# A hybrid encoder layer: the second pair's substitution, its values and the attention's projections in another order, the projection in three parts

## The chip, the cores and the metric

The kernel runs on one core of a Trainium2 chip. The metric is the device time of one execution in microseconds (us); the kernel before takes 1764.89 us, the median of three runs between 1764.22 and 1765.56.

The engines that matter are TensorE (PE in the profile, its weight loads PEld), VectorE (DVE), ScalarE (ACT), GpSimd (POOL) and SyncE (SP), which issues nearly all of this kernel's DMAs. Each engine carries out its own instructions strictly in the order in which the program lists them, and so does each queue of DMA issues: an instruction that waits holds up all that is listed behind it on its engine.

## What is computed

One layer of an encoder, applied with the same weights to a prompt of 1024 tokens and a sample of 256 (1280 tokens, ten tiles of 128). After a norm, one projection feeds two head groups. Group A is a bidirectional gated DeltaNet with four heads; group B is grouped-query attention with four query heads and two key-value heads, with a norm and an axial rotary position on queries and keys.

```python
h = _rmsnorm(x, norm_mix_pre)
p = h @ w_in
qkv_a, z_a, b_f, b_b, a_f, a_b, q_b, k_b, v_b = _split_cols(p)
o_a = _gated_deltanet(qkv_a, z_a, b_f, b_b, a_f, a_b, ...)
o_b = _axial_gqa(q_b, k_b, v_b, q_norm_w, k_norm_w)
mix = jnp.concatenate([o_a, o_b], axis=-1) @ w_out
x = x + _rmsnorm(mix, norm_mix_post)
hm = _rmsnorm(x, norm_mlp_pre)
f = jnp.square(jax.nn.relu(hm @ w_up)) @ w_down
return x + _rmsnorm(f, norm_mlp_post)
```

Inside the DeltaNet, every chunk needs a triangular solve, `tri = eye + strict(k_beta k^T * decay)`, per head, chunk and direction. The kernel builds the inverse of each triangle: 32x32 blocks on the diagonal by substitution, row by row, and then the blocks off the diagonal by small matmuls.

## The kernel before

All products are made in three matmuls of high and low parts (`hi*hi`, `hi*lo`, `lo*hi`), so one projection of 128 columns over 1280 tokens (`proj_T`, L351 to L369) is 72 matmuls: 48 of 512 columns and 24 of 256, in three blocks of tokens, each of which ends with a copy of its PSUM tile to SBUF by ScalarE (L369).

The execution has these stages: the norm and the z gate's projection; the **preparation** of DeltaNet and attention, from about 105 to 571 us of the trace; the DeltaNet's steps with the attention beside them, 571 to 799 us; the output projection; and the MLP, to the end.

In the preparation, generators are advanced one after the other by a string, `ORDER`. A letter names a generator and a digit its head, pair or projection; each mention runs it up to its next `yield`:

- `K0`..`K3`, `gdn_qk`: two projections, convolution, transposes and norms of a head's queries and keys.
- `V0`..`V3`, `gdn_v`: the same for its values.
- `E0`..`E3`, `gdn_e`: decay factors and k k^T products of a head, five pairs of chunks. It fills the matrix `C` and writes `A` (one buffer, L538) to DRAM (L544, L545).
- `S0`, `S1`, `gdn_sub`: the substitution of heads 0 and 1, or 2 and 3. It starts with a round trip of the diagonal blocks through DRAM (`c_d`, L564 to L567); then come 31 pairs of a product (L575, tile `prod`) and an update (L577, tile `Rm`) on VectorE, each dependent on the one before, with a memset on GpSimd (L578).
- `L0`..`L3`, `gdn_lev`: a head's blocks off the diagonal. It takes `Rm` through DRAM (`r_d` L585, `Rc` L589), transposes it on VectorE (`Rt` L592) and makes two levels of small matmuls (L605 to L617, L634 to L641); the finished `C` goes to DRAM (L645, L646).
- `a0`..`a7`, `att_proj`: the attention's projections, four of queries (`a0`..`a3`), two of keys (`a4`, `a5`), two of values (`a6`, `a7`). `a0`..`a5` write the projection to DRAM (L390) and load it back with halves of its rows exchanged (`axw`, four DMAs, L393); ten transposes (L399) feed sums of squares on ScalarE (L375); VectorE makes the reciprocal root in 13 small steps (L89 to L99) and four multiplications with the rotary table (L414 on the projection, L415 on `axw`); GpSimd adds the two (L416); keys are scaled by ten small matmuls (`prk`, L422) and VectorE (L425); the result goes to DRAM (L429).

The order in the string gives each instruction its place; the program's scheduler then orders the instructions of each engine by it, so neighbours in the string are interleaved.

Several buffers are few, and a step that needs one waits until its last user is done. The projection's result `araw` and the convolution's input share two buffers (tag `cp`, L387). `axw` and the convolution's output share one (tag `cy`). `A` has one. Three PSUM tiles serve all projections (`mm`). The buffers of the preparation as a whole (`gp`) are given up only when its last instruction has read them; the loads of the DeltaNet's steps (`vis`, L668) take the same memory.

Of the kernel before, what the change touches and what calls it, by code (L numbers as in the profile page):

```python
# [37 lines left out]


ORDER = (  # L40
# [3 lines left out]
)  # L44


# [16 lines left out]
def build(ctx, tc, I, O):  # L63
# [19 lines left out]
    def rsqrt(p, out, ss, n, inv_n, tag, x_out=None):  # L83

        x = x_out if x_out is not None else p.tile([128, n], F32, tag=f"{tag}x", name=f"{tag}x")
        xh = p.tile([128, n], F32, tag=f"{tag}h", name=f"{tag}h")
        y = p.tile([128, n], F32, tag=f"{tag}y", name=f"{tag}y")
        t = p.tile([128, n], F32, tag=f"{tag}t", name=f"{tag}t")
        V.tensor_scalar(x, ss, inv_n, EPS, ALU.mult, ALU.add)  # L89
        V.tensor_scalar(xh, x, -0.5, None, ALU.mult)  # L90
        V.tensor_scalar(t.bitcast(I32), x.bitcast(I32), 1, None, ALU.logical_shift_right)
        V.tensor_scalar(y.bitcast(I32), t.bitcast(I32), -1.0, MAGIC, ALU.mult, ALU.add)
        for i in range(3):
            if n == 1:
                V.scalar_tensor_tensor(t, y, xh, y, ALU.mult, ALU.mult)
            else:
                V.tensor_tensor(t, y, y, ALU.mult)
                V.tensor_tensor(t, t, xh, ALU.mult)
            V.scalar_tensor_tensor(out if i == 2 else y, t, 1.5, y, ALU.add, ALU.mult)  # L99
# [253 lines left out]
    def proj_T(c, dst, segs):  # L353
        wts = []
        for g in range(2):
            raw = tp_.tile([128, 4, 128], F32, tag="wraw", name="wraw", bufs=2)
            SP.dma_start(out=raw, in_=w_in[g * 512:(g + 1) * 512, c:c + 128].rearrange("(k p) c -> p k c", p=128))
            whi = tp_.tile([128, 4, 128], F32R, tag="whi", name="whi", bufs=3)
            wlo = tp_.tile([128, 4, 128], F32R, tag="wlo", name="wlo", bufs=3)
            split(whi, wlo, raw)  # L360
            wts.append((whi, wlo))
        for t0, n, c0 in segs:
            pm = mm_tile("pt")
            for k in range(KD):
                whi, wlo = (w[:, k % 4] for w in wts[k // 4])
                T.matmul(pm[:, :n], lhsT=whi, rhs=h_hi[:, k, t0:t0 + n], start=(k == 0), stop=False)  # L366
                T.matmul(pm[:, :n], lhsT=whi, rhs=h_lo[:, k, t0:t0 + n], start=False, stop=False)  # L367
                T.matmul(pm[:, :n], lhsT=wlo, rhs=h_hi[:, k, t0:t0 + n], start=False, stop=(k == KD - 1))  # L368
            S.copy(dst[:, c0:c0 + n], pm[:, :n])  # L369

    def sum_sq(p, tp, n, ss):

        for j in range(n):
            junk = p.tile([128, 128], BF16, tag="gj", name="gj", bufs=1)
            S.activation(junk, tp[:, j * 128:(j + 1) * 128], AF.Square, accum_out=ss[:, j:j + 1])  # L375
# [3 lines left out]
    def att_proj(j):  # L379

        if not att and j < 6:
            rope = gp.tile([128, 2, 1282], F32, tag="qk", name="rope", bufs=2)[:, :, 0:1024]
            SP.dma_start(out=rope, in_=I["c_rope"])
            att[0] = rope
        rope = att.get(0)
        c = (2064 + j * 128, 2576 + (j - 4) * 128, 2832 + (j - 6) * 128)[max(0, j - 2) // 2]
        raw = tp_.tile([128, TOK], F32, tag="cp", name="araw", bufs=2)  # L387
        proj_T(c, raw, ((0, 512, 0), (512, 512, 512), (1024, 256, 1024)))
        if j < 6:
            SP.dma_start(out=aqkv_d[j], in_=raw)  # L390
            xw = tp_.tile([128, TOK], F32, tag="cy", name="axw", bufs=1)
            for b in range(4):
                SP.dma_start(out=xw[b * 32:b * 32 + 32], in_=aqkv_d[j][(b ^ 1) * 32:(b ^ 1) * 32 + 32])  # L393
        yield
        for t0 in range(0, NT, 4):
            n = min(4, NT - t0)
            tp = at_tile("at")
            for i in range(n):
                T.transpose(tp[:, i * 128:(i + 1) * 128], raw[:, (t0 + i) * 128:(t0 + i + 1) * 128], ident)  # L399
            if j < 6:  # L400
                sum_sq(gp, tp, n, ssa[:, j, t0:t0 + n])
            else:
                cs = slice(t0 * 128, (t0 + n) * 128)
                vn = gp.tile([128, 512], F32, tag="kn", name="avn", bufs=3)[:, :n * 128]
                S.copy(vn, tp[:, :n * 128])
                SP.dma_start(out=arot_d[j][:, cs], in_=vn)
        if j >= 6:
            return
        rs = rsa[:, j]
        rsqrt(gp, rs, ssa[:, j], NT, 1.0 / 128, "na")  # L410
        w = nw[:, j // 4]
        for c0, n in ((0, 1024), (1024, 256)):
            cs = slice(c0, c0 + n)
            V.scalar_tensor_tensor(raw[:, cs], raw[:, cs], w[:, 0:1], rope[:, 0, :n], ALU.mult, ALU.mult)  # L414
            V.scalar_tensor_tensor(xw[:, cs], xw[:, cs], w[:, 1:2], rope[:, 1, :n], ALU.mult, ALU.mult)  # L415
        G.tensor_tensor(raw, raw, xw, ALU.add)  # L416
        if j >= 4:
            for t0 in range(0, NT, 4):
                n = min(4, NT - t0)
                pr = at_tile("prk")  # L420
                for i in range(n):
                    T.matmul(pr[:, i * 128:(i + 1) * 128], lhsT=rs[:, t0 + i:t0 + i + 1].to_broadcast([128, 128]), rhs=ident,  # L422
                             start=True, stop=True)
                cs = slice(t0 * 128, (t0 + n) * 128)
                V.tensor_tensor(raw[:, cs], raw[:, cs], pr[:, :n * 128], ALU.mult)  # L425
        else:
            V.tensor_scalar(rs, rs, scale, None, ALU.mult)
            V.tensor_scalar(nsa[:, j], rs, -1.0, None, ALU.mult)
        SP.dma_start(out=arot_d[j], in_=raw)  # L429
# [152 lines left out]
    def gdn_lev(h):  # L582
# [63 lines left out]
        SP.dma_start(out=vis_d[h][:, :, 8], in_=C[:, :, 0])  # L646

    FN = dict(K=gdn_qk, V=gdn_v, E=gdn_e, S=gdn_sub, L=gdn_lev, a=att_proj)
    parts = {}
    for step_ in ORDER.split():  # L650
# [666 lines left out]
    for s, (n, i) in enumerate(seq):  # L1317
# [20 lines left out]
        if s > 9 and (s - 10) % 4 == 0 and s < 38:  # L1338
            j = UP[(s - 10) // 4][1]
# [171 lines left out]
```

## Time and profile before

| | us |
|---|---|
| median of three runs | 1764.89 (1764.22 to 1765.56) |
| the profiled execution, its own time | 1767.37 |
| its span in the trace | 1765.6 |
| outside the span | 1.8 |
| PE busy in the span | 1633.7 (93%) |
| DVE busy | 1244.3 (70%) |
| ACT busy | 875.8 (50%) |
| POOL busy | 697.8 (40%) |

The profile is one execution. Its page gives busy times over the whole span; the windows view gives busy time of each engine in a stretch of time, with the clock that TensorE was granted (1 is full speed); the timeline gives single instructions, with the idle time before one and what ended it in brackets; the groups view sums instructions of one line and kind; the waits view lists who waited for whom. A line number such as L575 is one of the kernel before, unless the changed kernel is spoken of: there the lines of `att_proj` from L395 on, and all behind it, have moved by up to two.

### The profile page before, as it was taken

How to read it: one execution, taken by the hardware profiler on the slowest of the kernel's cores; microseconds unless marked ns; L12 is line 12 of the kernel's file. 1: busy time of each engine (PE TensorE's matmuls, PEld its weight loads, DVE VectorE, ACT ScalarE, POOL GpSimd, SP SyncE). 2: the span in 40 equal slices, each digit the busy share in tenths (PEclk: the TensorE clock that was granted, in tenths of full speed). 3: DMA queues.
4: the chain of work that ended last, by engine and by line, in shares of the span. 5: the costliest groups of instructions: out<-in, count | busy, mean ns of one | idle time of the engine just before them, and what ended most of it. 6: DMA issues, size and time to landing. Idle time of an engine off the chain costs nothing. (4 is left out here: it accounts for less than half of the span.)

```text
span 1765.6 us, 27828 instructions
## 1 busy us (share of the span) xinstructions
PE 1633.7 (93%) x9799; PEld 1401.9 (79%) x9799; DVE 1244.3 (70%) x2425; ACT 875.8 (50%) x2017; POOL 697.8 (40%) x574
## 2 busy tenths in 40 slices
PE   6999998997856999989998999999989999999997
PEld 5778887776744878767877899999988788888885
DVE  6557559736857687886668955544777888887777
ACT  5237747565226676775446654545556333333422
POOL 3201011101114243530001465445635777888663
PEclk9999999998877999999999999999999999999999
DMA  6113434255444876444333444343565544444334
GB/s 208 66 45 108 132 84 121 73 150 152 139 126 135 276 234 205 135 152 141 128 111 127 160 165 144 127 136 129 184 210 194 171 145 135 135 141 138 98 111 154
DMA packets 208778, 252.67 MB, mean 143 GB/s; under 512 B 35073, under 2 KB 163391, under 8 KB 208639
## 3 DMA queue, kind: packets, MB, share of 16 engines
q1 hardware_dynamic: 208495, 250.77, 44.7%
q8 instruction: 77, 1.26, 0.3%
q14 instruction: 62, 0.51, 0.1%
q0 software_dynamic: 144, 0.13, 0.0%
HBM read 159.75 MB, written 91.10 MB: 142 GB/s over the span
## 5 line engine op out<-in xcount | busy, mean ns | idle before, releaser
L1162 PE MATMUL pd<-mh,ulo 128*128 128x320 f32 x892 | 280.1, 314 | 12.9 <-DVE ulo L81 12.9
L1161 PE MATMUL pd<-mh,uhi 128*128 128x320 f32 x892 | 277.1, 311 | 5.0 <-ACT uhi L80 5.0
L1163 PE MATMUL pd<-ml,uhi 128*128 128x320 f32 x892 | 277.6, 311 | 0.0
L1305 DVE TENSOR_TENSOR acc<-acc,pd 128x512 f32<-128x512 f32 x330 | 206.8, 679 | 43.9 <-PE pd L1301 43.9
L1299 PE MATMUL pd<-dhi,fhi 128*128 128x512 f32 x490 | 192.4, 393 | 1.4 <-DVE acc L1307 1.4
L1300 PE MATMUL pd<-dl,fhi 128*128 128x512 f32 x490 | 192.5, 393 | 0.0
L1301 PE MATMUL pd<-dhi,flo 128*128 128x512 f32 x490 | 192.0, 392 | 0.0
L1162 PEld LDWEIGHTS pd<-mh,ulo 128*128 128x128 f32 x892 | 169.6, 190 | 17.9 <-DVE ulo L81 17.9
L366 PE MATMUL pt<-h_hi,whi 128*128 128x512 f32 (+1 forms) x480 | 177.1, 369 | 0.0
L367 PE MATMUL pt<-h_lo,whi 128*128 128x512 f32 (+1 forms) x480 | 175.6, 366 | 0.0
L368 PE MATMUL pt<-h_hi,wlo 128*128 128x512 f32 (+1 forms) x480 | 175.1, 365 | 0.4 <-DVE wlo L81 0.4
L1161 PEld LDWEIGHTS pd<-mh,uhi 128*128 128x128 f32 x892 | 169.4, 190 | 6.3 <-ACT uhi L80 6.2
L1163 PEld LDWEIGHTS pd<-ml,uhi 128*128 128x128 f32 x892 | 169.5, 190 | 0.0
L1281 ACT CAST fhi<-fr 128x1280 fp32r<-128x1280 f32 x49 | 62.1, 1268 | 212.1 <-PE pd L1300 116.6
L81 POOL TENSOR_TENSOR dl<-dw,dhi 128x1024 fp32r<-128x1024 f32 x49 | 129.0, 2632 | 43.4 <-ACT dhi L80 42.8
L1206 POOL TENSOR_TENSOR s<-u,u 128x320 f32<-128x320 f32 x32 | 35.5, 1108 | 208.6 <-ACT u L1171 141.8
L743 POOL TENSOR_TENSOR P<-P,sm 128x512 f32<-128x512 f32 (+1 forms) x72 | 72.6, 1027 | 96.5 <-DVE sm L741 67.4
L1299 PEld LDWEIGHTS pd<-dhi,fhi 128*128 128x128 f32 x490 | 92.0, 188 | 22.6 <-DVE acc L1307 1.9
L81 DVE TENSOR_TENSOR ulo<-us,uhi 128x512 fp32r<-128x512 f32 x88 | 77.9, 887 | 43.9 <-ACT uhi L80 43.1
L1301 PEld LDWEIGHTS pd<-dhi,flo 128*128 128x128 f32 x490 | 92.0, 188 | 20.8
L1300 PEld LDWEIGHTS pd<-dl,fhi 128*128 128x128 f32 x490 | 92.0, 188 | 20.4
L368 PEld LDWEIGHTS pt<-h_hi,wlo 128*128 128x128 f32 x480 | 91.8, 191 | 15.0 <-DVE wlo L81 0.9
(358 smaller groups left out, 4092.0 us busy)
## 6 DMA issues: line engine op xcount, KB each, us to landing
fr<-r_d SPq DMA_DIRECT2D x49, 640.0 KB
vis<-vis_d SPq DMA_DIRECT2D x64, 384.0 KB
uraw<-in_w_up SPq DMA_DIRECT2D x22, 1024.0 KB
r_d<-s SPq DMA_DIRECT2D x128, 160.0 KB
r_d<-u SPq DMA_DIRECT2D x96, 160.0 KB
dw<-in_w_down SPq DMA_DIRECT2D x28, 512.0 KB
wraw<-in_w_in SPq DMA_DIRECT2D x48, 256.0 KB
x<-in_x_prompt SPq DMA_DIRECT2D x16, 512.0 KB
```

Of the source, the lines that this page charges most:

```text
L81: (V if leng is None else leng).tensor_tensor(lo, src, f32(hi), ALU.subtract)
L366: T.matmul(pm[:, :n], lhsT=whi, rhs=h_hi[:, k, t0:t0 + n], start=(k == 0), stop=False)
L367: T.matmul(pm[:, :n], lhsT=whi, rhs=h_lo[:, k, t0:t0 + n], start=False, stop=False)
L368: T.matmul(pm[:, :n], lhsT=wlo, rhs=h_hi[:, k, t0:t0 + n], start=False, stop=(k == KD - 1))
L743: G.tensor_tensor(x[:, :kw], x[:, :kw], sm[:, 0:1].to_broadcast([128, kw]), ALU.mult)
L1161: T.matmul(pm, lhsT=w[0][:, k], rhs=mh[b, i][:, k], start=(k == 0), stop=False)
L1162: T.matmul(pm, lhsT=w[1][:, k], rhs=mh[b, i][:, k], start=False, stop=False)
L1163: T.matmul(pm, lhsT=w[0][:, k], rhs=ml[b, i][:, k], start=False, stop=(k == 3))
L1299: T.matmul(pm, lhsT=r[0][:, k, tk], rhs=w[0][:, k], start=(k == 0), stop=False)
L1300: T.matmul(pm, lhsT=r[0][:, k, tk], rhs=w[1][:, k], start=False, stop=False)
L1301: T.matmul(pm, lhsT=r[1][:, k, tk], rhs=w[0][:, k], start=False, stop=(k == Q - 1))
L1305: V.tensor_tensor(half(t, d), half(t, d), pm, ALU.add)
```

## The change

Two things are changed: the string `ORDER`, and the places at which `att_proj` yields.

```diff
@@ -38,9 +38,9 @@
 ORDER = (
-    "K0 K0 K0 V0 K0 K0 V0 E0 K1 E0 V0 E0 E0 K1 E0 K1 a6 K1 K1 a6 E1 a7 E1 E1 a7 E1 E1 V1 S0 K2 S0 V1 S0 K2 S0 V1 S0 K2 "
-    "S0 K2 S0 K2 S0 K3 L0 L0 K3 L1 L1 E2 V2 E2 K3 E2 K3 E2 V2 K3 E2 V2 V3 E3 E3 V3 E3 a4 E3 V3 E3 a4 S1 a5 S1 a5 S1 a0 "
-    "S1 S1 a0 S1 a1 S1 S1 a1 L2 L2 a2 L3 L3 a2 a3 a3"
+    "K0 K0 K0 V0 K0 K0 V0 E0 K1 E0 V0 E0 E0 K1 E0 K1 a6 K1 K1 a6 E1 E1 V1 E1 E1 E1 S0 K2 S0 V1 S0 K2 S0 V1 S0 K2 "
+    "S0 K2 S0 K2 S0 K3 L0 L0 K3 L1 E2 L1 K3 a7 E2 E2 K3 E2 K3 E2 a7 E3 V2 E3 E3 V2 E3 E3 S1 V2 V3 S1 S1 V3 S1 a4 S1 "
+    "V3 S1 a4 S1 a5 S1 a4 L2 a5 L2 a0 L3 a5 L3 a0 a1 a0 a1 a2 a1 a2 a3 a2 a3 a3"
 )
@@ -388,10 +388,11 @@
         proj_T(c, raw, ((0, 512, 0), (512, 512, 512), (1024, 256, 1024)))
         if j < 6:
             SP.dma_start(out=aqkv_d[j], in_=raw)
+        yield
+        if j < 6:
             xw = tp_.tile([128, TOK], F32, tag="cy", name="axw", bufs=1)
             for b in range(4):
                 SP.dma_start(out=xw[b * 32:b * 32 + 32], in_=aqkv_d[j][(b ^ 1) * 32:(b ^ 1) * 32 + 32])
-        yield
         for t0 in range(0, NT, 4):
             n = min(4, NT - t0)
             tp = at_tile("at")
@@ -406,6 +407,7 @@
                 SP.dma_start(out=arot_d[j][:, cs], in_=vn)
         if j >= 6:
             return
+        yield
         rs = rsa[:, j]
         rsqrt(gp, rs, ssa[:, j], NT, 1.0 / 128, "na")
         w = nw[:, j // 4]
```

`att_proj` has now three parts for queries and keys: the projection and its write to DRAM; the load of `axw`, the transposes and the sums of squares; and the reciprocal root, the rotary multiplications, the scaling and the write. In the string, `a7` goes from amid `E1` to behind `K3`; the pairs of `E2` and `E3` follow one another with `V2` begun only inside `E3`; `S1` stands with `V2`, `V3`, `a4` and `a5` instead of `a5`, `a0` and `a1`; and `a5` to `a3` are staggered behind and between `L2` and `L3`. The number of instructions on each engine is the same before and after (8823 on PE, 2427 on DVE, 1707 on ACT, 579 on POOL, 825 on SP, as the programs list them).

On VectorE, around the eighth to tenth step of `S1` (`prod` and `Rm` are the substitution's product and update; `araw`, `axw` and `prk` are the attention projection's), the kernel before has these instructions:

```order
L575 TENSOR_TENSOR prod<-Rm 80x2x192
L415 SCALAR_TENSOR_TENSOR axw<-axw,nw,rope 128x1024
L415 SCALAR_TENSOR_TENSOR axw<-axw,nw,rope 128x256
L577 TENSOR_TENSOR Rm<-Rm,prod 80x2x24x8
L575 TENSOR_TENSOR prod<-Rm 80x2x207
L577 TENSOR_TENSOR Rm<-Rm,prod 80x2x23x9
L425 TENSOR_TENSOR araw<-araw,prk 128x512 x2
L425 TENSOR_TENSOR araw<-araw,prk 128x256
L575 TENSOR_TENSOR prod<-Rm 80x2x220
L81 TENSOR_TENSOR wlo<-wraw,whi 128x512
L577 TENSOR_TENSOR Rm<-Rm,prod 80x2x22x10
L414 SCALAR_TENSOR_TENSOR araw<-araw,nw,rope 128x1024
```

and the changed kernel these, from the eighth step to the twelfth:

```order
L577 TENSOR_TENSOR prod<-Rm 80x2x192
L579 TENSOR_TENSOR Rm<-Rm,prod 80x2x24x8
L577 TENSOR_TENSOR prod<-Rm 80x2x207
L579 TENSOR_TENSOR Rm<-Rm,prod 80x2x23x9
L577 TENSOR_TENSOR prod<-Rm 80x2x220
L579 TENSOR_TENSOR Rm<-Rm,prod 80x2x22x10
L417 SCALAR_TENSOR_TENSOR axw<-axw,nw,rope 128x1024
L577 TENSOR_TENSOR prod<-Rm 80x2x231
L417 SCALAR_TENSOR_TENSOR axw<-axw,nw,rope 128x256
L579 TENSOR_TENSOR Rm<-Rm,prod 80x2x21x11
L577 TENSOR_TENSOR prod<-Rm 80x2x240
L427 TENSOR_TENSOR araw<-araw,prk 128x512
```

Before, the rotary work of `a4`, `a5`, `a0` and `a1` stands inside `S1`; in the changed kernel only one rotary step on `axw` and one scaling, both of `a4`, and later a rotary step of `a5`. Of GpSimd's adds (L416, in the changed kernel L418), three stand inside `S1` before and one after.

On SP's queue, around the end of `S1` (`r_d` carries the substitution's result to DRAM, `Rc` brings it back for `L2` and `L3`, `arot_d` is a finished projection, `ax` the attention's own loads), the kernel before has these issues:

```order
L429 DMA arot_d<-araw 128x1280
L393 DMA axw<-aqkv_d 32x1280 x4
L390 DMA aqkv_d<-araw 128x1280
L429 DMA arot_d<-araw 128x1280
L393 DMA axw<-aqkv_d 32x1280 x2
L585 DMA r_d<-Rm 80x1024
L393 DMA axw<-aqkv_d 32x1280
L589 DMA Rc<-r_d 32x20x32 x4
L393 DMA axw<-aqkv_d 32x1280
L585 DMA r_d<-Rm 80x1024
L390 DMA aqkv_d<-araw 128x1280
L679 DMA ax<-arot_d 128x512 x2
```

and the changed kernel these:

```order
L587 DMA r_d<-Rm 80x1024 x2
L591 DMA Rc<-r_d 32x20x32 x8
L647 DMA vis_d<-C 1280x1x128
L648 DMA vis_d<-C 1280x1x128
L395 DMA axw<-aqkv_d 32x1280 x4
L431 DMA arot_d<-araw 128x1280
L647 DMA vis_d<-C 1280x1x128
L648 DMA vis_d<-C 1280x1x128
L390 DMA aqkv_d<-araw 128x1280
L431 DMA arot_d<-araw 128x1280
L395 DMA axw<-aqkv_d 32x1280 x4
L390 DMA aqkv_d<-araw 128x1280
```

Before, five projections (`a4`, `a5`, `a0`, `a1`, `a2`) have their `axw` loaded ahead of `L2` or beside its start, and the attention's own loads begin there. In the changed kernel `a0`'s `axw` load is the first behind `L2`'s result, and three more projections' round trips (write `aqkv_d`, load `axw`, write `arot_d`) stand behind that of `L3`. The matmuls follow: of the 576 projection matmuls of `a0` to `a7`, 576 stand ahead of `L2`'s first on PE before, and 432 after (`a2` and `a3` behind `L3`). Ahead of `E2`'s first k k^T product stand 44 fewer projection matmuls than before (31 fewer of `a4`'s, and none of `a5`'s 13); that product now follows `L1`'s first level (`px`) directly. The attention's score products begin amid `L3` before, and behind `a3`'s last transposes after.

## The prediction

> **What bounds the kernel now.** I read the windows by stage first, since the busy shares of the whole span hide where PE waits.
>
> ```profile
> core 0: us, PE busy (x) PEld busy (x) DVE busy (x) ACT busy (x) POOL busy (x), PEclk, DMA share, GB/s
> 196.75:426.00 229.25, 212.97 (x1576) 174.26 (x1575) 148.72 (x296) 135.44 (x369) 25.04 (x60) 0.94 0.42 117
> 426.00:571.50 145.50, 95.60 (x945) 78.61 (x943) 103.01 (x238) 59.04 (x198) 32.18 (x49) 0.81 0.44 129
> 571.50:799.00 227.50, 212.94 (x1310) 174.34 (x1310) 173.89 (x530) 156.08 (x455) 91.75 (x112) 0.97 0.59 198
> ```
>
> Up to 426 us and from 571.5 us PE is busy 93 and 94% of the time. Between them, where the change works, it is busy 95.6 of 145.5 us: a chain sets the pace. The chain is read from the timeline, engine by engine: E3's last pair, S1's round trip and its first and last steps, L2, L3, the last projection's rotary step, and the first load of the DeltaNet's steps.
>
> ```profile
> 424.33 0.42 DVE L540 TENSOR_TENSOR A<-E,pk 128x256 f32<-128x256 f32 x1 [4.69 <-DMA vis_d<-A]
> 438.68 0.35 SPq L429 DMA_DIRECT2D arot_d<-araw  x1
> 439.48 0.83 SPq L564 DMA_DIRECT2D c_d<-Ct  x1
> 443.52 2.06 SPq L567 DMA_DIRECT2D Rm<-c_d  x4
> 448.63 0.22 DVE L575 TENSOR_TENSOR prod<-Rm 80x62 f32<-80x62 f32 x1 [3.60 <-DMA axw<-aqkv_d]
> 503.67 0.30 SPq L585 DMA_DIRECT2D r_d<-Rm  x1
> 506.56 1.97 SPq L589 DMA_DIRECT2D Rc<-r_d  x4
> 522.75 1.76 ACT L644 ACTIVATE C<-py 64x320 f32<-64x320 f32 x4 [0.65 <-PE py L641]
> 532.55 0.92 ACT L622 COPY C<-Rt 32x320 f32<-32x320 f32 x2 [0.32 <-DVE Rt L592]
> 543.10 1.78 ACT L644 ACTIVATE C<-py 64x320 f32<-64x320 f32 x4
> 568.90 2.53 DVE L415 SCALAR_TENSOR_TENSOR axw<-axw,nw,rope 128x1024 f32<-128x1024 f32 x2
> 571.50 0.80 SPq L668 DMA_DIRECT2D vis<-vis_d  x2
> ```
>
> So E3 ends at 426.1, S1 runs from 448.6 to 503.6 (55.0 us), L2 is done 21 us later, L3 at 544.9, and the steps' first load leaves at 571.5, in the moment at which the last rotary multiplication is read out and the preparation's memory is free. From S1's end to that load: 67.9 us.
>
> **The change, part by part.** The sum is made on the profiled execution (1767.4 us, span 1765.6); the shift it gives is then laid on the median, 2.5 us lower.
>
> *E2 and E3 earlier.* E2's first pair starts at 374.0, and there DVE had waited for PE:
>
> ```profile
> 374.04 0.42 DVE L540 TENSOR_TENSOR A<-E,pk 128x256 f32<-128x256 f32 x1 [6.47 <-PE pk L539]
> 470.00:490.00 20.00, 20.00 (x94) 16.91 (x93) 20.00 (x50) 5.82 (x25) 4.26 (x11) 0.88 0.44 145
> DVE A L540 <- DMA vis_d<-A: 20.1, 9, 4.7
> ```
>
> In a stretch full of projections PE makes 94 matmuls in 20.00 us, 0.213 us each. The 44 projection matmuls that no longer stand ahead of that pair are 9.4 us, ten transposes that go as well some 2 us, and the pair need not wait for L1's second level, about 4 us by the 12.3 us that L3 takes for both levels (532.6 to 544.9). That is 15 to 16 us. From the first pair to E3's end the kernel takes 52.1 us for ten pairs, with 20.1 us in all of waits for A's write. With V2 and V3 mostly out from among the pairs I expect 2 us less: E3's end 18 us earlier, at 408. The bounds are 9 us (only PE's matmuls count, and the waits for A stay) and 20 us.
>
> *S1's start.* Before it comes 22.5 us behind E3's end. The arot write of a4 kept SP until 438.68 and c_d behind it. It goes, but a4's own rotary work and 13 root steps now stand on DVE ahead of the first product. I take 2 us off; between 0 and 6 (SP's wait counted in full) is possible.
>
> *S1 itself.* What goes from inside it:
>
> ```profile
> L575 DVE TENSOR_TENSOR prod<-Rm 80x62 f32<-80x62 f32 (+15 forms) x31 | 21.4, 689 | 4.1 <-DMA axw<-aqkv_d 3.6
> L577 DVE TENSOR_TENSOR Rm<-Rm,prod 80x62 f32<-80x62 f32 (+15 forms) x31 | 16.1, 520 | 0.5
> 457.12 3.22 DVE L575 TENSOR_TENSOR prod<-Rm 80x414 f32<-80x414 f32 x1
> 456.83 3.05 POOL L416 TENSOR_TENSOR araw<-araw,axw 128x1280 f32<-128x1280 f32 x1 [1.62 <-DVE axw L415]
> 477.13 3.11 POOL L416 TENSOR_TENSOR araw<-araw,axw 128x1280 f32<-128x1280 f32 x1 [2.47 <-DVE axw L415]
> 495.89 3.20 POOL L416 TENSOR_TENSOR araw<-araw,axw 128x1280 f32<-128x1280 f32 x1 [2.50 <-DVE prod L575]
> ```
>
> The updates cost 16.1 us, the products 5.3 us more, and the product at 457.12 takes 3.22 us while GpSimd's add runs. Three adds fall into S1; the excess over 16.1 us divides into 1.8 us each. Taking two adds out is worth 3.5 to 5.3 us. The rotary multiplications, scalings and root steps of three projections go too: 55.0 less 37.5 us of S1's own leaves 17.5 us of foreign work, of which one rotary pair, a scaling, two or three splits and gaps of the dependent chain stay, about 11. So S1 takes 45 us, between 41 and 50, and ends at 408 + 20.5 + 45 = 473.5, which is 30 us earlier.
>
> *What follows S1.* L2's chain (503.67 to 524.5, 20.8 us) and L3's second part (12.3 us) stay, since Rc of L3 is now loaded right behind L2's: 33 us. But PE no longer has a2 and a3 behind it. Their 144 matmuls at 0.213 us are 30.7 us, behind L3. Behind a3's last matmul come its copy, its write and reload, and the rotary step; the rows that price these:
>
> ```profile
> 480.27 0.33 SPq L429 DMA_DIRECT2D arot_d<-araw  x1
> 480.82 2.31 SPq L393 DMA_DIRECT2D axw<-aqkv_d  x4
> 484.02 1.08 ACT L369 COPY araw<-pt 128x512 f32<-128x512 f32 x2 [9.48 <-DMA arot_d<-araw]
> 502.52 1.35 ACT L369 COPY araw<-pt 128x512 f32<-128x512 f32 x3 [14.90 <-DMA arot_d<-araw]
> L415 DVE SCALAR_TENSOR_TENSOR axw<-axw,nw,rope 128x1024 f32<-128x1024 f32 (+1 forms) x10 | 9.4, 962 | 0.0
> ```
>
> Copies 1.35, a write 2.9 (as r_d to Rc, 503.67 to 506.56), the reload 2.3 for its issues and some 2.7 to land, two multiplications 1.9: 11 us. The least is 33 + 31 + 11 = 75 us. The copies of a2 and a3 wait for an araw buffer, that is for a0's and a1's writes to DRAM: such waits were 9.48 and 14.90 us before, beside a busy PE. Here they also hold the PSUM tiles, and with them PE. I add 7 us, something under a third of the 24.4 us that they make together: 82 us, against 67.9 before. The bounds are 75 and 93 (with 18 us of those waits, the rest beside L3). The steps' first load then leaves at 473.5 + 82 = 555.5, 16 us earlier than before.
>
> *What is given back.* Before 571.5 PE had already worked on the attention:
>
> ```profile
> L728 PE MATMUL ps_s<-k_hi,q_hi 128*128 128x512 f32 x13 | 7.1, 549 | 1.8 <-ACT P L737 1.6 <-ACT q_hi L80 0.2
> L730 PE MATMUL ps_s<-k_hi,q_lo 128*128 128x512 f32 x13 | 6.8, 520 | 0.0
> L729 PE MATMUL ps_s<-k_lo,q_hi 128*128 128x512 f32 x13 | 6.5, 500 | 0.0
> L751 PE MATMUL ptr<-ident,P 128*128 128x128 f32 x8 | 2.0, 338 | 7.5 <-POOL P L743 7.5
> ```
>
> 39 score matmuls, 8 transposes and one product: 48 by 0.213 us is 10.2 us. After the change PE comes to these only behind a3, so they go into the stage that is 94% full and lengthen it by as much. The first waits of a softmax (7.5 us on POOL's P above), so far spent in the preparation, come back there beside the steps' work; I take 3 us, from 0 to 7.5. Net: -16 + 10.2 + 3 = about -3. From 1764.9 that is 1762.
>
> *The clock.* The windows also hold TensorE's granted clock.
>
> ```profile
> 490.00:510.00 20.00, 11.47 (x61) 9.29 (x59) 13.61 (x29) 1.95 (x5) 4.19 (x11) 0.89 0.35 93
> 510.00:530.00 20.00, 8.30 (x280) 7.74 (x280) 7.45 (x16) 7.98 (x18) 0.00 (x0) 0.59 0.55 155
> ```
>
> Around L2 the clock falls to 0.59 while PE is busy 8.3 of 20 us. In the sum, a2 and a3 run at the 0.213 us of a stretch with clock 0.88, which charges 144 x 0.213 x (1 - 0.88/0.97), 2.8 us, for that. The Trainium skill ("TensorE: Matmul & The Clock Gate", section "What's actually happening") says that the clock is halved after an idle window of about 3.4 us and is back after as long a busy one. By that, an estimate from that page's figures: each of the two projections, if PE stood idle before it, would lose half of 3.4 us, 3.4 us together, and my sum would move by under 1 us; the rule speaks against this change, which puts projections behind gaps, but not strongly.
>
> **The rivals.** *The drain is short* (faster). E3 ends 20 us earlier, S1 takes 43, and a2 and a3 flow behind L3 with 76 us to the first load: 2 + 2 + 6 us more than the forecast, so -13, 1752; with half of it 1757. I price it at 1754. For it: behind L3 only the projections' own instructions are left on ScalarE and VectorE. Against: the forecast's drain of 82 us already has but 7 us of waiting in it.
>
> *The staggered projections are a serial chain* (slower). One axw buffer and two araw buffers serve a0 to a3, and the adds that end a step are spaced like this: 456.83, 477.13, 495.89, so 19 to 20 us each. a5's add falls between L2 and L3, at about S1's end + 24 us; four more steps follow. The forecast's 82 us leave (82 - 24)/4 = 14.5 us for each step. Above that, every us counts four times: at 17 us the load leaves 10 us later than forecast, which gives 1772; at the full 19.5 us it is 1782. For it: before, these steps ran ahead of S1's end, where they cost nothing, and now they are at the end of the path. Against: the spacing was partly S1's own work on DVE between the rotary steps.
>
> *The order does not bring E2 forward* (slower). A single A buffer and DVE's other work keep E3's end at 9 us earlier; the rest as forecast: 9 us more, 1771.
>
> **How the numbers follow.** A measurement of this kernel tells some 0.2%, 3.5 us, from no change. Near the forecast, -8 to +4 us: 0.46, of which 0.15 lie below -3.5, 0.26 within, 0.05 above. The short drain 0.24, all faster. The serial chain 0.22 and E2 not forward 0.08, all slower. Together faster 0.39, same 0.26, slower 0.35. The likeliest case gives 1762, its own range 1757 to 1769. The range for 8 in 10 takes in the short drain down to 1750 and the serial chain up to 17 or 18 us a step, 1776.
>
> **What would show it.** Right: E3's last pair near 408 us, S1's 62 steps in about 45 us with one product of some 3 us, the steps' first load near 555 us, no score matmul on PE before it, and the stage after it about 240 us long instead of 227.5. Wrong: E3's end above 415 (E2 not forward); adds on POOL behind S1 spaced by over 15 us (serial chain); under 77 us from r_d to the first load (short drain); or a stage of the steps that is no longer than before although the head start is gone, in which case the term of 13 us was not owed.

## The result and the profile after

The changed kernel takes 1782.78 us (median of four runs, 1779.10 to 1784.86), the kernel before on the same chip 1765.22 (1764.22 to 1769.48). The ratio is 1.0093, with a 95% interval of 1.0069 to 1.0116: slower, and outside the range that was forecast. The profiled execution took 1783.51 us, with a span of 1781.7.

The chain in the timeline of the changed kernel, by the same steps as before (E3's last pair, S1's round trip, its first product and its end, the loads for L2 and L3, the first load of the attention, the first load of the DeltaNet's steps):

```profile
414.80 0.42 DVE L542 TENSOR_TENSOR A<-E,pk 128x256 f32<-128x256 f32 x1 [2.02 <-DMA vis_d<-A]
422.14 0.33 SPq L567 DMA_DIRECT2D c_d<-Cc  x1
425.26 3.52 SPq L569 DMA_DIRECT2D Rm<-c_d  x4
435.53 0.22 DVE L577 TENSOR_TENSOR prod<-Rm 80x62 f32<-80x62 f32 x1
485.25 0.78 SPq L587 DMA_DIRECT2D r_d<-Rm  x2
488.29 12.36 SPq L591 DMA_DIRECT2D Rc<-r_d  x8
556.77 0.34 SPq L681 DMA_DIRECT2D ax<-arot_d  x1
568.43 0.80 SPq L670 DMA_DIRECT2D vis<-vis_d  x2
```

E3 ends at 416.6 us (9.5 earlier than before), S1 starts at 435.5 (13.1 earlier) and ends at 485.2 (18.4 earlier), and the steps' load leaves at 568.4: only 3.1 us earlier. So 15 of the 18 us are lost again between S1's end and that load.

The larger part of the loss comes behind that load. The attention's first score and last value product, as the tile views give them, first for the kernel before:

```profile
L728 PE MATMUL ps_s<-k_hi,q_hi x72: 282/476/797, 534.2 to 794.0; 128*128 128x512 f32 x64, 128*128 128x256 f32 x8
L757 PE MATMUL po<-p_hi,v_lo x72: 281/394/629, 572.8 to 814.3; 128*128 128x512 f32 x64, 128*128 128x256 f32 x8
```

and for the changed kernel:

```profile
L730 PE MATMUL ps_s<-k_hi,q_hi x72: 363/475/796, 568.6 to 814.7; 128*128 128x512 f32 x64, 128*128 128x256 f32 x8
L759 PE MATMUL po<-p_hi,v_lo x72: 278/393/632, 596.5 to 832.2; 128*128 128x512 f32 x64, 128*128 128x256 f32 x8
```

The first score comes 34.4 us later, the last value product 17.9 us later. From the steps' load to that product it is 242.8 us before (571.5 to 814.3) and 263.8 after: 21.0 us more. What follows takes 1.8 us less (951.3 before, 949.5 after). The sum, -3.1 + 21.0 - 1.8, is the 16.1 us by which the spans differ.

The windows view of the changed kernel, cut at E3's end, at the steps' load and at the output projection's first matmul (799.6 before, 815.1 after):

```profile
416.60:568.43 151.83, 92.13 (x959) 78.62 (x958) 86.81 (x209) 56.15 (x196) 21.76 (x38) 0.77 0.41 121
568.43:815.10 246.67, 222.28 (x1360) 181.48 (x1361) 198.95 (x560) 168.74 (x483) 102.34 (x121) 0.97 0.58 193
568.43:600.00 31.57, 26.11 (x143) 20.16 (x143) 23.05 (x44) 19.39 (x61) 16.40 (x13) 0.87 0.77 248
780.00:800.00 20.00, 14.49 (x65) 9.64 (x63) 15.41 (x28) 17.90 (x33) 7.17 (x6) 0.97 0.71 268
```

In the stage of the steps PE is busy 222.3 us instead of 213.5 (571.5 to 799.6 before), which is attention work that used to lie ahead of it, and idle 24.4 us instead of 14.6. Part of the idle time is at the start (5.5 us in the first 31.6), part in the stretch where the steps are done and the attention is alone. Cut at the steps' last product (757.8 before, 762.1 after), the 21.0 us divide so: from the load to that product 186.3 us before and 193.6 after, so 7.4 more, and from there to the last value product 56.6 and 70.2, so 13.6 more.

The waits view of PE and of ACT between E3's end and the steps' load, and rows of the timeline that say when the waits fell:

```profile
PE pt L366 <- ACT araw L369: 27.7, 2, 20.4
PE ph L607 <- DVE Rt L594: 14.7, 2, 11.1
PE ps_s L730 <- ACT q_hi L80: 10.8, 1, 10.8
...
ACT araw L369 <- DMA arot_d<-araw: 22.9, 2, 19.2
...
444.56 0.69 DVE L81 TENSOR_TENSOR wlo<-wraw,whi 128x512 fp32r<-128x512 f32 x1 [6.71 <-ACT whi L80]
465.13 1.35 ACT L369 COPY araw<-pt 128x512 f32<-128x512 f32 x3 [19.20 <-DMA arot_d<-araw]
524.74 0.78 PE L400 MATMUL at<-ident,araw 128*128 128x128 f32 x4 [3.75 <-ACT araw L369]
525.17 0.78 PE L366 MATMUL pt<-h_hi,whi 128*128 128x512 f32 x1
549.82 0.59 ACT L369 COPY araw<-pt 128x512 f32<-128x512 f32 x1 [3.66 <-DMA arot_d<-araw]
556.46 0.28 PE L368 MATMUL pt<-h_hi,wlo 128*128 128x256 f32 x1
```

PE waited 27.7 us for PSUM tiles that ScalarE had not emptied, and ScalarE 22.9 us for an araw buffer, that is for a finished projection's write to DRAM. Nearly all of this lies ahead of S1's end: PE's two waits end at 424.1 and 465.8, and the 19.2 us of ScalarE end at 465.1, where a0's result had waited for the buffer of a4. Behind S1's end PE waits 3.75 us for a1's copies, at 524.7, and ScalarE 3.7 us for a buffer, at 549.8, beside a busy PE. The last projections are late because a2's and a3's matmuls stand behind L3 in PE's order: the first starts at 525.17, and the last at 556.46 instead of 501.64 before. The attention's first load leaves at 556.77, right behind it. Inside S1 VectorE stood still for 6.71 us at a weight split, with the substitution's next step queued behind it.

### The profile page after: what moved, and what is told of

The parts are those of the page before. It is cut to its first block, busy times and chain, and to the rows that moved or that the text cites. A ratio compares the mean times of both kernels' runs of the same rounds, so it can differ in the third digit from the quotient of the medians.

```text
span 1781.7 us, 27832 instructions
## 1 busy us (share of the span) xinstructions
PE 1623.5 (91%) x9799; PEld 1395.8 (78%) x9799; DVE 1247.8 (70%) x2425; ACT 875.4 (49%) x2017; POOL 699.2 (39%) x574
## 5 line engine op out<-in xcount | busy, mean ns | idle before, releaser
L1164 PE MATMUL pd<-mh,ulo 128*128 128x320 f32 x892 | 279.7, 314 | 12.9 <-DVE ulo L81 12.9
L366 PE MATMUL pt<-h_hi,whi 128*128 128x512 f32 (+1 forms) x480 | 177.7, 370 | 27.7 <-ACT araw L369 27.7
L1164 PEld LDWEIGHTS pd<-mh,ulo 128*128 128x128 f32 x892 | 169.3, 190 | 17.9 <-DVE ulo L81 17.7
L366 PEld LDWEIGHTS pt<-h_hi,whi 128*128 128x128 f32 x480 | 92.2, 192 | 42.6 <-ACT araw L369 28.5
L1301 PEld LDWEIGHTS pd<-dhi,fhi 128*128 128x128 f32 x490 | 92.0, 188 | 22.1 <-DVE acc L1309 1.2
```

Of the source, the lines that this page charges most:

```text
L1164: T.matmul(pm, lhsT=w[1][:, k], rhs=mh[b, i][:, k], start=False, stop=False)
L1301: T.matmul(pm, lhsT=r[0][:, k, tk], rhs=w[0][:, k], start=(k == 0), stop=False)
```

## The experiments

Theory 1, from these two traces: the time is set by when the attention starts, and it starts late because the last projections are late. Its rival, theory 2: the first load of the DeltaNet's steps sets the time, and a head start of the attention is hidden work. The table gives, for each kernel, the lengths between the events above, read from the same rows of its profiled execution; "head start" is the steps' first load less the first score product. The profiled execution is one run, and the kernel before took 1759.1 to 1772.1 us over 34 runs, so a difference of a few us between two profiles is not a verdict; the ratio's interval is.

| kernel | E3's end to S1 | S1 | S1's end to load | load to last value product | head start | median, us | ratio to before (95%) |
|---|---|---|---|---|---|---|---|
| before | 22.5 | 55.0 | 67.8 | 242.8 | 37.3 | 1765 to 1767 | |
| changed | 18.9 | 49.7 | 83.2 | 263.8 | -0.2 | 1782.78 | 1.0093 (1.0069 to 1.0116) |
| x1_a0_last | 22.1 | 55.5 | 53.8 | 270.2 | -14.2 | 1781.59 | 1.0089 (1.0067 to 1.0111) |
| x13_a0_a2 | 22.1 | 55.4 | 54.2 | 263.2 | 0.1 | 1770.30 | 1.0023 (1.0003 to 1.0043) |
| x2_split | 22.3 | 55.1 | 69.0 | 246.9 | 39.5 | 1771.47 | 1.0043 (1.0027 to 1.0058) |
| x3_front | 18.5 | 66.5 | 68.1 | 260.8 | 11.7 | 1780.38 | 1.0088 (1.0060 to 1.0116) |
| x4_tail | 11.1 | 41.9 | 84.7 | 263.9 | -0.3 | 1785.91 | 1.0114 (1.0084 to 1.0144) |
| x7_after_own_a0a1 | 19.0 | 50.2 | 100.4 | 242.7 | 46.0 | 1780.20 | 1.0076 (1.0046 to 1.0106) |
| x9_before_own_a0a1 | 21.4 | 54.5 | 67.8 | 244.7 | 48.4 | 1769.01 | 1.0010 (0.9994 to 1.0027) |
| x6_after_a5_fourth | 18.9 | 49.7 | 92.2 | 265.3 | 1.7 | 1786.74 | 1.0109 (1.0080 to 1.0138) |
| x8_after_wlo_pool | 17.9 | 44.0 | 83.9 | 264.2 | -0.2 | 1775.45 | 1.0046 (1.0027 to 1.0064) |
| x10_before_wlo_pool | 25.9 | 53.7 | 65.2 | 244.1 | 28.5 | 1771.18 | 1.0021 (1.0006 to 1.0037) |
| x11_before_add_dve | 23.4 | 52.7 | 67.0 | 242.0 | 36.7 | 1765.05 | 0.9995 (0.9978 to 1.0012) |
| x12_before_both | 24.2 | 52.7 | 66.4 | 242.1 | 37.0 | 1765.06 | 0.9996 (0.9981 to 1.0011) |

**The head start alone.** In the order of the kernel before, the names a0 and a3 are exchanged; every other step stays where it is. The attention's first scores need a0.

```diff
-... S1 a5 S1 a5 S1 a0 S1 S1 a0 S1 a1 S1 S1 a1 L2 L2 a2 L3 L3 a2 a3 a3
+... S1 a5 S1 a5 S1 a3 S1 S1 a3 S1 a1 S1 S1 a1 L2 L2 a2 L3 L3 a2 a0 a0
```

> The kernel before with the names a0 and a3 exchanged in its order: the preparation has the same work in the same places, but the projection that the attention's first scores need is now the last one, so its head start is gone. Theory 1 (the stage behind the preparation is set by when the attention starts, 534 us before and 568.6 us in the changed kernel): the first load of the DeltaNet's steps leaves no later than 571.5 us, first score product at 560 us or later, out-projection's first matmul 10 to 18 us later than 799.6, time 1774 to 1783. Theory 2 (the load of the steps sets the time, the head start is hidden work): time within 5 us of the kernel before, 1760 to 1770.

The load and the first score of this kernel:

```profile
561.13 0.81 SPq L668 DMA_DIRECT2D vis<-vis_d  x2
L728 PE MATMUL ps_s<-k_hi,q_hi x72: 282/473/796, 575.3 to 810.7; 128*128 128x512 f32 x64, 128*128 128x256 f32 x8
L757 PE MATMUL po<-p_hi,v_lo x72: 278/394/480, 602.1 to 831.3; 128*128 128x512 f32 x64, 128*128 128x256 f32 x8
```

The preparation is the same and the steps' load leaves 10 us earlier than before, yet the kernel is as slow as the changed one. Theory 2 is out as a full account. The table's column from S1's end to the load shows a second thing: without the attention beside it, that way takes 53.8 instead of 67.8 us. GpSimd's adds of the last two rotary steps show where, first in the kernel before, then in this one:

```profile
547.34 2.88 POOL L416 TENSOR_TENSOR araw<-araw,axw 128x1280 f32<-128x1280 f32 x1
571.51 2.90 POOL L416 TENSOR_TENSOR araw<-araw,axw 128x1280 f32<-128x1280 f32 x1 [1.56 <-DVE sm L740]
```

```profile
549.61 2.89 POOL L416 TENSOR_TENSOR araw<-araw,axw 128x1280 f32<-128x1280 f32 x1 [42.47 <-DVE araw L414]
561.30 2.88 POOL L416 TENSOR_TENSOR araw<-araw,axw 128x1280 f32<-128x1280 f32 x1 [8.80 <-DVE axw L415]
```

They lie 24.2 us apart where VectorE has the softmax's instructions between the steps' own, and 11.7 where it has not. The head start of before is not free: it makes the load 14 us later, and it gives back 27 us behind it (270.2 against 242.8).

**Half of the head start.** The same with a0 and a2 exchanged.

> The kernel before with a0 and a2 exchanged in its order: the attention's first queries are finished as the last but one projection instead of the last (a0 and a3 exchanged) or the third (before). Two-term theory, from the runs so far: the attention's last value product ends 243 to 247 us behind the first load of the steps where the attention has 37 us or more of head start on that load, 261 where it has 12, 264 where it has none and 270 where it starts 14 us later. Here the first score should come near 555 us with 5 to 15 us of head start, the attention's end 258 to 264 us behind the load, time 1772 to 1780. Rival (only the load of the steps counts, and x1 was slower for another reason): end 243 to 247 us behind the load, time 1756 to 1766.

The first score comes with the load (561.0 and 561.1), not 5 to 15 us ahead of it, and the last value product 263.2 us behind it: what the changed kernel shows with no head start. The median is just below the expected range. Against before, 14 us less on the way to the load and 20 more behind it leave a small loss, 1.0023: on balance the head start of 37 us is worth some 4 us here.

**Front and tail of the order apart.** The first kernel has the changed order up to E3's end and then the tail of before; the second has the order of before up to E3's end and then the changed tail.

```diff
 x3_front: changed order up to "... E3 V2 E3 E3 V2 E3 E3", att_proj in two parts, then
+S1 V2 V3 V3 a4 V3 a4 a5 S1 a5 S1 a0 S1 S1 a0 S1 a1 S1 S1 a1 L2 L2 a2 L3 L3 a2 a3 a3
 x4_tail: order of before up to "... E3 E3 V3 E3 a4 E3 V3 E3", att_proj in three parts, then
+S1 S1 S1 S1 a4 S1 S1 S1 a5 S1 a4 L2 a5 L2 a0 L3 a5 L3 a0 a1 a0 a1 a2 a1 a2 a3 a2 a3 a3
```

> The changed order up to the end of E3 (a7 behind K3, E2 and E3 ahead of V2 and V3), then the tail of the kernel before, with a5, a0 and a1 inside S1, att_proj in two parts. Theory 1 (the front is worth the 9.5 us by which E3 ends earlier in the changed kernel, the tail is the cost): E3's end near 417 us, attention's first score near 525 us, time 1755 to 1760, 5 to 10 us faster than the kernel before. Rival (the front's gain is lost again because V2 and V3 now stand ahead of S1's rotary work): within 3 us of the kernel before.

> The order of the kernel before up to the end of E3, without a4's second part, then the changed order's tail (S1 with little beside it, a4 and a5 late in it, a0 to a3 behind L2 and L3), att_proj in three parts. Theory 1 (front and tail add up; the front of the changed kernel hid 9.5 us of the tail's cost): 22 to 28 us slower than the kernel before, 1787 to 1793. Rival (the tail alone costs what the change cost, the front is worth nothing): 14 to 19 us slower, 1779 to 1784.

Both expectations of theory 1 missed, and for the first kernel its rival's too. The front's gain does not survive: E3 ends at 415.3, but S1 then takes 66.5 us. a4's rotary step, whose add stands ahead of S1 at 427.8 in the kernel before, now falls into it (450.8), beside a5's and a0's. That makes three adds, as in S1 of the kernel before (there a5's, a0's and a1's); what it has more is the scaling of a second key projection (3.4 us in all against 1.6) and a 6.59 us wait of a weight split for ScalarE. The rest of the 11.5 us was not traced. S1's first product and its end in that kernel:

```profile
433.81 0.22 DVE L575 TENSOR_TENSOR prod<-Rm 80x62 f32<-80x62 f32 x1
...
500.29 0.77 SPq L585 DMA_DIRECT2D r_d<-Rm  x2
```

S1 ends 3.4 us earlier than in the kernel before, the load leaves 3.2 us earlier, and the head start is 11.7 instead of 37.3 us, with 18.0 us more behind the load. From E3's end to the load this kernel needs 153.1 us and the changed one 151.8 (18.9 + 49.7 + 83.2): the rotary steps that stand in S1 here and behind it there cost 16.8 us in S1 (66.5 against 49.7) and 15.1 behind it (83.2 against 68.1). By these two kernels it makes little difference to the load on which side of S1's end they stand. The tail alone leaves out the head start (263.9) and shortens the way to the load by 7.6 us (137.7 against 145.3); its time lies between the two expectations, 20 us above before with runs from 1778.4 to 1789.9, and its profile is of the fastest of them. So front and tail do not add up: each alone costs the head start, or most of it.

**The split alone.** The order of before, att_proj in three parts, the second and third called together.

```diff
-... E3 V3 E3 a4 S1 a5 S1 a5 S1 a0 S1 S1 a0 S1 a1 S1 S1 a1 L2 L2 a2 L3 L3 a2 a3 a3
+... E3 V3 E3 a4 a4 S1 a5 S1 a5 a5 S1 a0 S1 S1 a0 a0 S1 a1 S1 S1 a1 a1 L2 L2 a2 L3 L3 a2 a2 a3 a3 a3
```

> The order of the kernel before, but att_proj in three parts, the second and third called one right after the other: what is left of the change is that axw is loaded at the second mention instead of the first. Theory 1 (the cost lies in the new order): within 3 us of the kernel before, 1762 to 1768. Rival (the later load of axw delays each rotary step by itself): 4 us per late step on the chain behind S1, 1769 to 1777.

Slower by 1.0043, which theory 1 did not allow and the rival's range did, though not by its mechanism: the way from S1's end to the load grows by 1.2 us only. 4.1 us come behind the load, where the instructions are the same and their order on the engines has changed with the preparation's. The waits view of that stage for this kernel and, below it, for the kernel before:

```profile
PE po L758 <- DVE p_lo L81: 7.7, 12, 1.8
```

```profile
PE po L756 <- DVE p_lo L81: 3.3, 8, 0.8
```

PE waits 4.4 us more for VectorE's splits of the probabilities. What in the order causes this was not tried.

**Why the projections are late.** Theory 3 was formed on the rows at 556.46 and 556.77: the attention's tiles take the memory of h, which is free behind the last projection matmul, and in the changed kernel that matmul is late for want of araw buffers. The edit gives a0 and a1 a buffer of their own.

```diff
-        raw = tp_.tile([128, TOK], F32, tag="cp", name="araw", bufs=2)
+        if j in (0, 1):
+            if 1 not in att:
+                att[1] = gp.tile([128, 2, 1282], F32, tag="qk", name="araw2", bufs=2)
+            raw = att[1][:, (0, 1).index(j), 0:TOK]
+        else:
+            raw = tp_.tile([128, TOK], F32, tag="cp", name="araw", bufs=2)
```

> The changed kernel with one thing more: a0's and a1's results lie in a buffer of their own (the second one of tag qk, free once E3 has read its keys), so the two buffers that a4 and a5 use come to a2 and a3. Theory 3 (the attention takes over the memory of h, which is free only behind the last projection matmul; in the changed kernel the projections of a2 and a3 wait for araw buffers until 556 us, and that is what delays the attention and makes the time): all projections are done on PE before L2, the first ax load leaves by 520 us instead of 556.8, first score before 540 us, time 1752 to 1766, at least 15 us below the changed kernel's 1782. Theory 2 (the serial chain of rotary steps behind L2 and L3 sets the time): the first load of the steps stays at 565 us or later and the time within 6 us of 1782.

> The kernel before with the same buffer of their own for a0 and a1. Theory 3: the projections end a few us earlier (the copies waited 9.5 and 14.9 us for araw buffers), the attention's first scores move ahead of L3, and the time falls by 3 to 12 us, 1754 to 1763. Theory 2: the rotary steps inside S1 are unchanged and so is the first load of the steps, time within 3 us of the kernel before.

In the changed kernel with this buffer, these rows of SP's queue and of GpSimd's adds answer:

```profile
493.58 1.40 SPq L686 DMA_DIRECT2D ax<-arot_d  x3
551.90 18.43 SPq L686 DMA_DIRECT2D ax<-arot_d  x4
588.83 0.80 SPq L675 DMA_DIRECT2D vis<-vis_d  x2
...
546.52 2.45 POOL L423 TENSOR_TENSOR araw<-araw,axw 128x1280 f32<-128x1280 f32 x1 [15.00 <-DVE nat L98]
566.80 2.90 POOL L423 TENSOR_TENSOR araw<-araw,axw 128x1280 f32<-128x1280 f32 x1 [1.83 <-issue]
588.85 2.94 POOL L423 TENSOR_TENSOR araw<-araw,axw 128x1280 f32<-128x1280 f32 x1 [2.88 <-DVE axw L422]
```

The mechanism is shown: with the buffers the scheduler puts all the projections ahead of L2, the last one starts at 490.2, the attention's first load leaves at 493.6 instead of 556.8, the head start is 46 us and the stage behind the load is back at 242.7. Other kernels show the gate itself: in x3, x4, x8 and x9 the first attention load leaves 0.3 us behind the start of the last projection matmul (547.36 and 547.67 in x3, 492.52 and 492.83 in x9). In the changed kernel the buffers do not act as a wait of those matmuls but through their place behind L3. The time is not what theory 3 expected: it is 1780.2. With the attention now at work beside them, the last three rotary steps are spaced by 20 and 22 us, and the load comes at 588.8, 20 us later. That is theory 2's chain, and theory 2's ranges hold here (the load at 565 or later, the time within 6 us of 1782). Neither theory alone holds; the table's two columns together do. In the kernel before the same buffer takes the head start from 37 to 48 us and changes nothing that can be measured (1.0010), as theory 2 expected: in the seven kernels with 28 to 48 us of head start, the stage behind the load takes 242 to 247 us.

**Which data the attention waits for.** The changed kernel with the places of a5, a0 and a1 rotated: a0 takes a5's, a1 a0's, a5 a1's.

> The changed kernel with a5's place in the order given to a0, a0's to a1 and a1's to a5: keys and queries of the first scores are rotated one step earlier, and a5, which is needed late, one or two steps later. If the attention waits for its data (its first keys and queries): first score product 10 us or more earlier than 568.6 and time 6 to 12 us below 1782. Theory 3 (it waits for the memory of h, that is for the last projection matmul): first score between 562 and 570 us, time 1777 to 1785.

The first score comes at 576.7, later still, although a0's result was written 18 us earlier (SP's write at 509.1 against 527.1): it isn't its own keys and queries that the attention waits for in the changed kernel. Theory 3's two ranges missed as well, the time from above. Its gate opens as it says (last projection matmul at 558.64, first attention load at 559.74), but the load of the first queries leaves only at 571.9, on SP's queue behind another projection's write at 569.0 and reload at 569.5. The load of the steps comes 9 us later behind S1's end (92.2); that a5's scaling by `prk` now stands late in the chain may be why, but it was not tried.

**The wait inside S1.** The changed kernel with the low parts of a0's to a3's weights split on GpSimd.

```diff
-            split(whi, wlo, raw)
+            split(whi, wlo, raw, leng=G if 2064 <= c < 2576 else None)
```

> The changed kernel with the low parts of a0's to a3's weights (wlo) split on GpSimd instead of VectorE, which takes the 6.71 us wait of a split out of S1 on VectorE. Theory 3: S1 ends 5 to 7 us earlier, but the projections still wait for araw buffers, so the first load of the steps and the time fall by 2 to 7 us, 1775 to 1780. Theory 2 (S1's end sets everything behind it one to one): 6 to 8 us, 1774 to 1776; if GpSimd's splits hold up the substitution's steps instead: no gain.

S1 takes 44.0 us instead of 49.7 and ends 7.9 us earlier, all that follows keeps its length (83.9 and 264.2 against 83.2 and 263.8), and the median falls by 7.3 us, which lies in both theories' ranges. At an unchanged head start, what the way to S1's end loses goes nearly one to one into the time.

**Versions of the kernel before.** The same edit there, the add of a rotary step on VectorE instead of GpSimd, and both:

```diff
-        G.tensor_tensor(raw, raw, xw, ALU.add)
+        V.tensor_tensor(raw, raw, xw, ALU.add)
```

> The kernel before with the low parts of a0's to a3's weights split on GpSimd instead of VectorE. Two-term theory: S1 loses 3.4 us of splits on VectorE, and its end and the load of the steps come 2 to 4 us earlier, with the head start untouched: 1761 to 1764. Rival (what is taken from VectorE comes back as steps of the substitution held up by GpSimd, or as projections that end later): 1765 to 1769.

> The kernel before with the add at the end of a rotary step on VectorE instead of GpSimd. A product of the substitution takes 3.2 instead of 0.6 us while the add runs on GpSimd (2.6 us, three times in S1); two more adds of 2.9 us stand in the chain behind S1. On VectorE an add of 1280 elements should take about 1.5 us by the 1.27 us of a multiplication of 1024. Two-term theory: 1 us less per add in S1, 1.4 less per add behind, 4 to 6 us in all, 1759 to 1762. Rival (VectorE is the chain's engine, so every instruction moved to it costs in full): 1765 to 1769.

> Both of the last two edits on the kernel before. Two-term theory: 6 to 10 us faster than before, 1756 to 1760. Rival: no faster than the better one of the two.

None is faster by a measurable amount, and the first is slightly slower (1.0021), above both of its expected ranges; the other two fall where their rivals put them. The second does on VectorE what was expected of it, as S1's groups show:

```profile
L575 DVE TENSOR_TENSOR prod<-Rm 80x62 f32<-80x62 f32 (+15 forms) x31 | 16.1, 519 | 3.3 <-POOL Rm L569 2.9
L416 DVE TENSOR_TENSOR araw<-araw,axw 128x1280 f32<-128x1280 f32 x3 | 4.4, 1480 | 0.0
```

The products take 16.1 instead of 21.4 us, and three adds cost VectorE 4.4 us: 0.9 us of gain are left, and S1 was 2.3 us shorter in this profile. No version beats the kernel before.

## Why the prediction was wrong

The sum had two terms: the load 16 us earlier, and 13 us given back behind it. The signs of both were right; both sizes failed, and both in the direction that makes the kernel slower. Measured: 3.1 us earlier and 21.0 given back. Of the 12.9 us that the first term lacks, 8.5 are E3's and 4.7 S1's; the two other parts of it miss by 1.6 and 1.2 us and nearly cancel.

*E2 and E3 earlier: mis-sized, 8.5 us.* The step said 18 us, with 9 as its lower bound; E3 came 9.5 us earlier, which is the place of the third rival. Two parts of it failed. E2's first pair came 11.3 us earlier, not 15 to 16 (which of its three prices was too high stays open), and the next did not follow at the pace of before:

```profile
362.70 0.42 DVE L542 TENSOR_TENSOR A<-E,pk 128x256 f32<-128x256 f32 x1
...
368.61 0.69 DVE L532 TENSOR_TENSOR ER<-incl,gr 128x512 fp32r<-128x512 f32 x1 [4.12 <-PE pe L535]
372.08 0.42 DVE L542 TENSOR_TENSOR A<-E,pk 128x256 f32<-128x256 f32 x1 [2.78 <-PE pk L541]
```

It took 9.4 us (7.4 before, 374.04 to 381.48), because VectorE waited for PE's matmuls of the decay factors and of k k^T. What PE did between the two pairs, in its groups from 363 to 372 us, is the work that the first pair had overtaken, L1's second level and K3's transposes, beside 19 projection matmuls:

```profile
L465 PE MATMUL kt<-ident,qk 128*128 128x128 f32 x10 | 1.6, 290 | 0.3 <-ACT C L646 0.3
L636 PE MATMUL ph<-X,C 64*64 64x64 f32 x40 | 1.4, 220 | 0.0
L643 PE MATMUL py<-C,H 64*64 64x64 f32 x40 | 1.4, 220 | 0.0
```

A pair that is moved ahead alone gains nothing for the row of ten behind it. The pace of the ten, 53.9 us against 52.1, did not fall by 2 us either. VectorE's waits for A's write did fall, from 15.0 to 7.2 us in that stretch (the 20.1 us of the prediction are those from 196.75 us on), but its waits for PE rose from 5.0 to 12.4 us.

*S1's start: right,* 18.9 us behind E3's end against 20.5.

*S1: 49.7 us against 45, inside the bounds.* One product of 3.22 us was left, as forecast. What failed is the price of the splits that stay: by the rows they are work of 0.7 us each, and one of them held up VectorE for 6.71 us, since ScalarE's high part waited 11.05 us for PE's projection matmuls. The kernel with the splits on GpSimd shows it: 44.0.

*S1's end to the load: right, 83.2 us against 82.* L2 and L3 took 35.3 us against 33 (485.25 to 520.52, where L3's result leaves), from there to a2's first matmul 4.7 against the 7 put down for waits, a2's and a3's matmuls 31.6 against 31, and what follows them 11.7 against 11. For the 2.7 us in that last part, the landing of a reload, the prediction showed no row; a3's reload was ready 5.3 us behind its first issue (561.40 to 566.69), and 5.0 had been counted. The matmuls ran at a better clock than charged: a3's 72 took 14.1 us, 0.196 us each instead of 0.213, and PE was busy without a gap.

```profile
520.50:534.00 13.50, 9.70 (x40) 7.90 (x41) 11.32 (x35) 9.19 (x44) 2.91 (x1) 0.87 0.76 246
534.00:540.00 6.00, 6.00 (x33) 5.07 (x32) 0.17 (x1) 0.59 (x1) 0.00 (x0) 1.00 0.00 0
540.00:556.60 16.60, 16.60 (x98) 14.40 (x97) 7.88 (x22) 5.86 (x24) 4.82 (x2) 1.00 0.36 119
```

So the 2.8 us charged for a low clock were owed in part only: a2's 72 matmuls took 15.2 us (without a1's transposes between them), 1.1 us more than a3's, all of it at their start. By the rule cited from the Trainium skill ("TensorE: Matmul & The Clock Gate", section "What's actually happening"), the clock is back after a busy window of about 3.4 us. The rows agree, 0.87 in the window with gaps and 1.00 from 534 us on. What the prediction did not see is that the 67.9 us of before held 14 us of the attention's interference, as x1_a0_last shows with 53.8: the changed tail, which has no attention beside it, is not 15 but 29 us longer than what it replaces. The sum itself is not wrong by that, since it set 82 against the measured 67.9. But x13_a0_a2 tells what the loss of the head start costs on balance: its span is 7.2 us longer than that of the kernel before, and the changed kernel's is 8.9 us longer still, with a load 7.3 us later (568.4 against 561.1). By these profiles about half of the 16.1 us is the head start, and the rest the longer way to the load; by the medians (some 4 of 17 us for x13) the head start is the smaller part.

*Given back: mis-sized, 21.0 us against 13.2.* The 10.2 us of PE work moved as counted: from the load to the last value product PE is busy 238.9 us instead of 228.2. The idle time that came with it was put at 3 us and is 10.3 (24.9 against 14.6). It isn't the first wait of a softmax alone: 4.7 us of it fall into the first 28.5 us, and 4.3 behind the steps' end, where the attention now has 70.2 us to itself instead of 56.6. So the upper bound of 7.5 us, from the waits of one softmax, was too tight. That the price is the overlap lost to the end of the stage is a reading of these windows; the kernels with and without a head start show its size (243 against 263 to 270 us), not its parts.

The rivals: the short drain did not come. The serial chain priced 1772 to 1782 and the time is 1782.8, but not by its mechanism, so the match is luck: the way from S1's end to the load is 1.2 us longer than forecast, not 20. The five adds behind S1 start at 502.3, 524.2, 543.4, 554.7 and 568.7 us, 16.6 us apart on average where the forecast had 14.5, but the first comes 17 us behind S1's end instead of 24, and from 525 to 557 us PE's matmuls of a2 and a3 set the pace. E2 not forward came in size, with 9.5 us, though not for its reason, a single A buffer: the waits for that buffer fell.

## What to carry to other kernels

Work that starts early in a gap of PE has a price that its instruction count does not show: here 48 matmuls of 10 us were worth 20 us behind the load, and cost 14 us ahead of it. When a step of a chain is moved, follow its neighbours: an order that brings one stage forward by putting others behind it has moved a cost, and it's the sum to the next common event that counts. From E3's end to the load that is 145.3 us before and 151.8 after; without the attention beside it the old order needs 131 to 132 (x1, x13), so the new one is 20 us longer on this way. And look for the event that frees memory: a projection of 14 us at the end of a stage held up all that was to live in its input's place.

## What was not expected of the hardware

While GpSimd adds two tiles of 128x1280 (2.9 to 3.2 us), a VectorE product of 80x480 or so takes 3.22 us instead of 0.65; with the add on VectorE, where it takes 1.48 us, the products keep their length. The add is thus cheaper on the engine that it was taken from, though the kernel's time does not show it. Executions of one and the same program differ by up to 0.7% here (1759.1 to 1772.1 us over 34 runs).
